# Weight sums of an output projection: from VectorE in the stage to GpSimd in an earlier stage, through DRAM

## The chip, the cores and the metric

One Trainium2 chip, one of its cores; float32 throughout. The metric is the device time of one execution in microseconds (us), the median of the runs shown.

## What is computed

One step of a hybrid trunk layer for 640 tokens (512 of a prompt, 8 x 16 of samples): attention heads and a state-space group side by side, an output projection of both, a SwiGLU feed-forward and a gated embedding. What matters here, cut from the reference:

```python
a = rms_norm(x, g_mix)
proj = a @ w_in
...
merged = jnp.concatenate([rms_norm(attn, g_attn_out), rms_norm(ssm, g_ssm_out)], axis=-1)
h = x + merged @ w_out
f = rms_norm(h, g_ffn)
h = h + (jax.nn.silu(f @ w_gate) * (f @ w_up)) @ w_down
gate = jax.nn.sigmoid(rms_norm(h, g_ple) @ w_ple_gate)
h = h + gate * (p_i @ w_ple_proj)
```

`w_out` has 2048 x 2048 elements. `attn` is 8 heads of 128, `ssm` the gated output of the state-space group (GLU).

## The kernel before, in words

**Products.** Activations stand feature by token, so TensorE holds a 128x128 block of weights and streams 320 tokens. Every float32 operand is split into a high part and a rest (wh, wl of the weights; two planes of each activation), and one product is three matmuls, at L1231, L1232 (both wh) and L1233 (wl). The large projections go by Strassen's scheme in Winograd's form: a 2x2 block product takes seven products instead of eight. Four of the seven left operands are blocks' sums and differences of the weights (`winograd_weights`, L106), the right ones of the activations (`winograd_rows`, L115); `PRODUCTS` (L126) lists for each of the seven which weight operand (0 to 6) meets which activation operand. Operands 0 to 2 are blocks of the weights as they come, 3 to 6 the sums.

**Weights.** `Ring` streams them in units. A unit of the output projection is one [128, 1024] block of float32 (512 KB): four blocks of 256 columns. SyncE loads it to a staging tile wst (two of them, L60). `split` (L67) then has VectorE make the four sums ws (L109 to L112), ScalarE cast wst and ws to wh (L86) and VectorE take the rests wl (L87). wh and wl have two buffers each, ws one. A unit of kind 0 (not Strassen) is only split, at L77 and L78.

**Stages.** The state-space inputs (to about 200 us), v and the scan (to 326), the heads (326 to 658), GLU (663 to 755), the embedding's projection pj (755 to 790), the output projection o (790 to 1024.5), gate and up (to 2125), down, and the last projection p. In the heads TensorE's stream is `feature_major` (L760), the q and k products of one head after another; every four k-blocks it pumps `side` and `side2`, generators that issue the attention of the head before and the norms piece by piece. GLU is `feature_major` as well. The heads' loads stand on SyncE's queue in program order: weights wst, one-hot rows oh, values vp, cached keys kc (L887) and cached values vc (L896), two vc tiles per head that follow each other in one buffer.

**Output projection.** `mk` holds the eight right operands km0 to km7 (each with its seven combinations and its two planes), which `build` (L1082) makes: a load mb or bm, a scaling (L1085), casts (L1076 on ScalarE) and rests (L1077 on VectorE), the sums of rows by L118 to L121. Each of 8 columns j takes 4 units, 42 matmuls each, in `products` (L1219); `strassen` (L1252) then gathers the seven PSUM banks to ro, the residual is added (L1306), and c (L1293), h_dr (L1316) and fc_dr (L1196) follow. The order of instructions on each engine is fixed when the program is built, by a scheduler; an engine's queue is worked in that order, and an instruction that waits holds all behind it.

Of the kernel before, what the change touches and what calls it, by code (L numbers as in the profile page):

```python
# [42 lines left out]
class Ring:  # L43
# [4 lines left out]
    def __init__(self, nc, stage_pool, units):  # L48
        self.nc, self.units, self.sp = nc, units, stage_pool
        self.pool = None  # L50
        self.loaded, self.st, self.cut, self.pos = 0, {}, {}, 0

    def load(self, upto):
        while self.loaded < min(upto, len(self.units)):
            i = self.loaded
            _, src = self.units[i]
            t = self.sp.tile([P, W1], F32, tag="w_st", name=f"wst{i}", bufs=STAGE)
            n = src.shape[1]
            for part in self.parts(i, n):
                self.nc.sync.dma_start(t[:, part], src[:, part])  # L60
            self.st[i] = (t, n)
            self.loaded += 1

    def parts(self, i, n):
        return [slice(0, n // 2), slice(n // 2, n)] if i == 0 else [slice(0, n)]

    def split(self, i):  # L67
# [23 lines left out]

    def ahead(self):
        for j in (self.pos, self.pos + 1):
            if j < len(self.units) and self.units[j][0] == 1:
                self.split(j)

    def next(self):
        i = self.pos
        self.pos += 1
        self.split(i)  # L100
        if i + 1 < len(self.units) and self.units[i + 1][0] == self.units[i][0]:
# [63 lines left out]
def hybrid_step(ctx: ExitStack, tc: tile.TileContext, io):  # L165
# [7 lines left out]
    side, side2 = Side(), Side()  # L173
# [9 lines left out]
    units += [(1, io["w_out"][j, u]) for j in range(8) for u in range(4)]  # L183
# [23 lines left out]

    def act_tile(name):
        return ap_.tile([P, 7, NTOK], F32R, tag="act", name=name)

    def act_rows(name, n):

        ts = [act_tile(f"{name}{i}") for i in range(-(-2 * n // 7))]
        return [tuple(ts[(2 * k + i) // 7][:, (2 * k + i) % 7] for i in range(2)) for k in range(n)]
# [7 lines left out]
    warm = cp.tile([P, 1], F32, name="warm")  # L222
    nc.scalar.activation(warm, ones[:, 0:1], AF.Copy)

    def load_const(name, eng=nc.gpsimd):
        src = io[name]
        t = cp.tile(list(src.shape), F32, name="c_" + name)
# [53 lines left out]
    rtok = cp.tile([P, MT], F32, name="rtok")  # L281
    epsr = mp.tile([P, NTOK], F32, name="epsr")
    negc = mp.tile([40, NTOK], F32R, name="negc")
    negp = mp.tile([P, 512], F32R, name="negp")
# [252 lines left out]
    gffn = load_const("g_ffn")  # L537
    gple = load_const("g_ple")
# [221 lines left out]
    def feature_major(ps, ks, rate=1.0, start=True, stop=True, parts=None):  # L760

        n = len(ks)
        for u in range(0, n, 8):
            wh, wl = ring.next()
            for j in range(min(8, n - u)):
# [7 lines left out]
                if j % 4 == 3:  # L773
                    side2.pump(1.0)
                    side.pump(rate)
# [57 lines left out]
    def forget():  # L833
# [35 lines left out]
        nc.vector.memset(negc.bitcast(F32), 0.0)  # L869
# [6 lines left out]
    def loads(h):  # L876
        oh = tp.tile([P, 2, P], F32, tag="oh", name=f"oh{h}", bufs=1)
        ohr = tp.tile([P, 2, P], F32R, tag="ohr", name=f"ohr{h}", bufs=1)
# [155 lines left out]

    for h in range(H):
# [119 lines left out]
    build_early(4)  # L1155
    at.close()
# [23 lines left out]
    xp = open_top("ffn")  # L1180
    KB = 2
# [37 lines left out]
    def products(name, kps, after=None, order=None):  # L1219
# [4 lines left out]
        def product(i, u, cut):  # L1224
            a, b = PRODUCTS[i]
            wh, wl = cut
# [326 lines left out]
```

## Time and profile before

| | us |
|---|---|
| Runs: median of 3 (lowest, highest) | 2935.68 (2934.81, 2939.37) |
| The profiled execution's own time | 2942.17 |
| Its span | 2940.4 |
| TensorE busy in it (share) | 2828.1 (96%) |
| VectorE busy | 2241.3 (76%) |
| ScalarE busy | 1241.2 (42%) |
| GpSimd busy | 360.3 (12%) |

The profile is one execution; its span is the time between its first and last instruction. Matmuls are pipelined, so that a matmul's own duration (0.31 us) is longer than the distance to the next one. A group of instructions is one line, one engine and one operation; "idle before, releaser" is what ended the engine's wait. PE is TensorE, PEld its weight loads, DVE VectorE, ACT ScalarE, POOL GpSimd, SPq SyncE's queue of DMA issues.

### The profile page before, as it was taken

How to read it: one execution, taken by the hardware profiler on the slowest of the kernel's cores; microseconds unless marked ns; L12 is line 12 of the kernel's file. 1: busy time of each engine (PE TensorE's matmuls, PEld its weight loads, DVE VectorE, ACT ScalarE, POOL GpSimd, SP SyncE). 2: the span in 40 equal slices, each digit the busy share in tenths (PEclk: the TensorE clock that was granted, in tenths of full speed). 3: DMA queues.
4: the chain of work that ended last, by engine and by line, in shares of the span. 5: the costliest groups of instructions: out<-in, count | busy, mean ns of one | idle time of the engine just before them, and what ended most of it. 6: DMA issues, size and time to landing. Idle time of an engine off the chain costs nothing. (4 is left out here: it accounts for less than half of the span.)

```text
span 2940.4 us, 47366 instructions
## 1 busy us (share of the span) xinstructions
PE 2828.1 (96%) x19051; PEld 2716.3 (92%) x19051; DVE 2241.3 (76%) x3629; ACT 1241.2 (42%) x1628; POOL 360.3 (12%) x405
## 2 busy tenths in 40 slices
PE   8999999999889889999999999999999999999998
PEld 6889988887789889999999999999999999998898
DVE  7758254445688888888888888888887777899888
ACT  5343355556644453333333333333433344345433
POOL 1213300001000001101111111111110110100011
PEclk9999999999999999999999999999999999999999
DMA  5666734546545623232323333333555455647444
GB/s 174 168 187 179 244 118 169 182 156 239 205 141 180 240 98 125 95 124 96 119 101 118 102 118 102 118 102 118 205 145 148 135 158 170 164 158 273 136 158 140
DMA packets 137484, 449.16 MB, mean 153 GB/s; under 512 B 14096, under 2 KB 34672, under 8 KB 124464
## 3 DMA queue, kind: packets, MB, share of 16 engines
q1 hardware_dynamic: 120032, 396.47, 39.9%
q0 software_dynamic: 15936, 45.47, 6.1%
q10 hardware_dynamic: 1296, 4.20, 0.4%
q8 instruction: 149, 2.44, 0.3%
q14 instruction: 71, 0.58, 0.1%
HBM read 342.25 MB, written 101.18 MB: 151 GB/s over the span
## 5 line engine op out<-in xcount | busy, mean ns | idle before, releaser
L86 ACT ACTIVATE wh<-wst 128x768 fp32r<-128x768 f32 x328 | 276.9, 845 | 660.0 <-issue 320.0
L87 DVE TENSOR_TENSOR wl<-ws,wh 128x1024 fp32r<-128x1024 f32 x328 | 423.6, 1291 | 102.1 <-ACT wh L86 101.7
L86 ACT ACTIVATE wh<-ws 128x1024 fp32r<-128x1024 f32 x328 | 344.6, 1051 | 358.0 <-DVE ws L112 357.9
L87 DVE TENSOR_TENSOR wl<-wst,wh 128x768 fp32r<-128x768 f32 x328 | 334.3, 1019 | 169.8 <-ACT wh L86 169.7
L1231 PE MATMUL d<-kt,wh 128*128 128x320 f32 x1232 | 383.5, 315 | 11.7 <-ACT wh L86 5.4
L1231 PE MATMUL g<-kf,wh 128*128 128x320 f32 x1232 | 382.4, 311 | 5.5 <-ACT wh L86 5.3
L1232 PE MATMUL g<-kf,wh 128*128 128x320 f32 x1232 | 381.8, 310 | 0.0
L1232 PE MATMUL d<-kt,wh 128*128 128x320 f32 x1232 | 380.6, 312 | 0.0
L1231 PE MATMUL u<-kf,wh 128*128 128x320 f32 x1232 | 380.1, 309 | 0.0
L1233 PE MATMUL g<-kf,wl 128*128 128x320 f32 x1232 | 375.7, 310 | 4.5 <-DVE wl L87 4.5
L1232 PE MATMUL u<-kf,wh 128*128 128x320 f32 x1232 | 380.0, 309 | 0.0
L1233 PE MATMUL u<-kf,wl 128*128 128x320 f32 x1232 | 376.2, 309 | 0.1
L1233 PE MATMUL d<-kt,wl 128*128 128x320 f32 x1232 | 344.5, 315 | 7.3 <-DVE wl L87 7.3
L1231 PEld LDWEIGHTS d<-kt,wh 128*128 128x128 f32 x1232 | 234.9, 191 | 17.9 <-ACT wh L86 10.2
L1231 PEld LDWEIGHTS g<-kf,wh 128*128 128x128 f32 x1232 | 232.7, 189 | 6.8 <-ACT wh L86 6.8
L1233 PEld LDWEIGHTS g<-kf,wl 128*128 128x128 f32 x1232 | 230.3, 188 | 5.6 <-DVE wl L87 5.3
L1232 PEld LDWEIGHTS d<-kt,wh 128*128 128x128 f32 x1232 | 235.0, 191 | 0.0
L1233 PEld LDWEIGHTS d<-kt,wl 128*128 128x128 f32 x1232 | 224.7, 191 | 11.1 <-DVE wl L87 10.6
L1232 PEld LDWEIGHTS g<-kf,wh 128*128 128x128 f32 x1232 | 232.9, 189 | 0.0
L1231 PEld LDWEIGHTS u<-kf,wh 128*128 128x128 f32 x1232 | 231.3, 188 | 0.0
L1232 PEld LDWEIGHTS u<-kf,wh 128*128 128x128 f32 x1232 | 231.3, 188 | 0.0
L1233 PEld LDWEIGHTS u<-kf,wl 128*128 128x128 f32 x1232 | 230.2, 188 | 0.4 <-DVE wl L87 0.4
(488 smaller groups left out, 5878.4 us busy)
## 6 DMA issues: line engine op xcount, KB each, us to landing
wst<-in_w_gate SPq DMA_DIRECT2D x88, 512.0 KB
wst<-in_w_up SPq DMA_DIRECT2D x88, 512.0 KB
wst<-in_w_down SPq DMA_DIRECT2D x88, 512.0 KB
tc_dr<-t SPq DMA_DIRECT2D x22, 1120.0 KB
kt<-tc_dr SPq DMA_DIRECT2D x22, 1120.0 KB
wst<-in_w_qk SPq DMA_DIRECT2D x32, 512.0 KB
kc<-in_cache_k SPq DMA_DIRECT2D x16, 1024.0 KB
vc<-in_cache_v SPq DMA_DIRECT2D x16, 1024.0 KB
```

The source lines that it names most:

```text
L86: a = nc.scalar.activation(wh[:, part], x, AF.Copy)
L87: b = nc.vector.tensor_tensor(wl[:, part], x, wh[:, part].bitcast(F32), op=OP.subtract)
L1231: nc.tensor.matmul(ps[i], wh[:, a, w], k[:, 0, b], start=f, stop=False)
L1232: nc.tensor.matmul(ps[i], wh[:, a, w], k[:, 1, b], start=False, stop=False)
L1233: nc.tensor.matmul(ps[i], wl[:, a, w], k[:, 0, b], start=False, stop=l)
```

## The change

The 32 units of `w_out` become units of kind 2. Their four sums are made by GpSimd in 64 steps of a new generator, `sum_weights`, which is pumped beside `side2`: 56 pumps in heads 1 to 7, 16 in GLU. A step loads half the columns of a unit's four blocks ([128, 4, 128], 256 KB, rows of 512 bytes) into a tile `pre` (two buffers) on SyncE's queue, and the step after it makes the four sums in place on GpSimd and stores them to a DRAM tensor `s_dr` on GpSimd's queue. In the output projection a unit's blocks 1 to 3 are loaded (128x768), and the sums as two more tiles wt of 128x512, of which there are three buffers. wh and wl are then made in three parts (768, 512, 512 columns). The sums stand in another order, which `SUMS` maps. To find room, some constants move to a pool that ends before the output projection, and negc, negp and ohr into unused rows of an activation tile.

```diff
     def load(self, upto):
         while self.loaded < min(upto, len(self.units)):
             i = self.loaded
-            _, src = self.units[i]
+            kind, src = self.units[i]
+            src = src[0] if kind == 2 else src
             t = self.sp.tile([P, W1], F32, tag="w_st", name=f"wst{i}", bufs=STAGE)
             n = src.shape[1]
-            for part in self.parts(i, n):
+            for part in self.parts(i, n) if kind < 2 else [slice(256, n)]:
                 self.nc.sync.dma_start(t[:, part], src[:, part])
...
+    def load_sums(self, i):
+        if i < len(self.units) and self.units[i][0] == 2 and i not in self.sums:
+            self.sums[i] = []
+            for h in range(2):
+                s = self.pool_of_sums(2).tile([P, 2, 256], F32, tag="w_s2", name=f"wt{i}_{h}", bufs=3)
+                self.nc.sync.dma_start(s, self.units[i][1][1][:, 2 * h : 2 * h + 2])
+                self.sums[i].append(s)
...
-            s = self.pool.tile([P, 4, 256], F32, tag="w_s", name=f"ws{i}", bufs=1)
             q = t.rearrange("p (q n) -> p q n", q=4)
-            winograd_weights(nc, q, s)
-            for part, x in ((slice(0, 3), q[:, 1:]), (slice(3, 7), s)):
+            if self.units[i][0] == 1:
+                s = self.pool_of_sums(1).tile([P, 4, 256], F32, tag="w_s", name=f"ws{i}", bufs=1)
+                winograd_weights(nc, q, s)
+                parts = [(slice(3, 7), s)]
+            else:
+                self.load_sums(i)
+                parts = list(zip((slice(3, 5), slice(5, 7)), self.sums.pop(i)))
+            for part, x in [(slice(0, 3), q[:, 1:])] + parts:
                 a = nc.scalar.activation(wh[:, part], x, AF.Copy)
                 b = nc.vector.tensor_tensor(wl[:, part], x, wh[:, part].bitcast(F32), op=OP.subtract)
             self.done = (a.ins, b.ins)
-        self.cut[i] = (wh, wl)
+        self.cut[i] = (wh, wl) if self.units[i][0] == 0 else (wh, wl, SUMS[self.units[i][0]])
+        if self.units[i][0]:
+            self.load_sums(i + 1)
         self.load(i + 1 + STAGE)
...
+def winograd_weights_in_place(eng, q):
+
+    tt = eng.tensor_tensor
+    tt(q[:, 3], q[:, 0], q[:, 3], op=OP.add)
+    tt(q[:, 0], q[:, 1], q[:, 0], op=OP.subtract)
+    tt(q[:, 1], q[:, 3], q[:, 1], op=OP.subtract)
+    tt(q[:, 2], q[:, 2], q[:, 1], op=OP.subtract)
+
+
+
+SUMS = {1: (0, 1, 2, 3, 4, 5, 6), 2: (0, 1, 2, 6, 4, 3, 5)}
...
-    units += [(1, io["w_out"][j, u]) for j in range(8) for u in range(4)]
+    s_dr = dp.tile([32, P, 4, 256], F32, name="s_dr")
+    units += [(2, (io["w_out"][j, u], s_dr[4 * j + u])) for j in range(8) for u in range(4)]
...
                 if j % 4 == 3:
                     side2.pump(1.0)
+                    side3.pump(1.0)
                     side.pump(rate)
...
+    def sum_weights():
+
+        last = None
+        for i in range(65):
+            if i < 64:
+                n = slice(P * (i % 2), P * (i % 2) + P)
+                t = tp.tile([P, 4, P], F32, tag="pre", name=f"pre{i}", bufs=2)
+                nc.sync.dma_start(t, io["w_out"][i // 8, i // 2 % 4].rearrange("p (q n) -> p q n", q=4)[:, :, n])
+            if last is not None:
+                t_, i_, n_ = last
+                winograd_weights_in_place(nc.gpsimd, t_)
+                nc.gpsimd.dma_start(s_dr[i_][:, :, n_], t_)
+            last = t, i // 2, n
+            yield
+
+    side3.add(sum_weights())
     for h in range(H):
...
+    side3.drain()
     at.close()
     mid.close()
     psB.close()
...
         def product(i, u, cut):
             a, b = PRODUCTS[i]
-            wh, wl = cut
+            wh, wl, places = cut
+            a = places[a]
```

How the built order changes, at two places. In the rows of the changed kernel the line numbers are its own: L62 is L60 of before, L920 is L879, L923 is L882, L928 is L887, L937 is L896, and L1083 is the load of a pre tile.

SyncE's queue in the heads, where one head's cached values and the next weights are issued. Before:

```order
L60 DMA wst_4510<-in_w_qk 128x1024 [waits DMAHW7_49,DVE_49]
L60 DMA wst_4637<-in_w_qk 128x1024 [waits DMAHW0_49,DVE_49]
L882 DMA vp_4691<-v_dr 128x5x128 [waits DMAHW4_49,PE_49]
L896 DMA vc_1_4565<-in_cache_v 128x2048 [waits DMAHW5_49,PE_49]
L896 DMA vc_0_4693<-in_cache_v 128x2048 [waits DMAHW6_49,DMAHW5_49,PE_49]
L60 DMA wst_4729<-in_w_qk 128x1024 [waits DMAHW2_49,DVE_49]
L887 DMA kc_0_4772<-in_cache_k 128x2048 [waits PE_49]
```

And in the changed kernel (DMASW is a store on GpSimd's queue):

```order
L62 DMA wst_5256<-in_w_qk 128x1024 [waits DMAHW5_49,DMAHW2_49,DVE_49]
L923 DMA vp_5331<-v_dr 128x5x128 [waits PE_49]
L1083 DMA pre_5227<-in_w_out 128x4x128 [waits DMAHW0_49,DMASW7_49,Pool_49]
L937 DMA vc_1_5185<-in_cache_v 128x2048 [waits PE_49]
L1083 DMA pre_5282<-in_w_out 128x4x128 [waits DMAHW1_49,DMAHW6_49,DMASW0_49,Pool_49]
L62 DMA wst_5369<-in_w_qk 128x1024 [waits DMAHW7_49,DVE_49]
L1083 DMA pre_5321<-in_w_out 128x4x128 [waits DMAHW4_49,DMASW1_49,Pool_49]
L937 DMA vc_0_5333<-in_cache_v 128x2048 [waits DMAHW5_49,PE_49]
```

Loads of pre tiles now stand ahead of the cached values and between the weights, and each of them waits for a store on GpSimd's queue.

VectorE's queue ahead of the output projection, where the first unit's wl is made (wl_7751 before; wl_8190 after). Before:

```order
L1077 TENSOR_TENSOR km_7186<-mb_7184,km_7186 128x320
L111 TENSOR_TENSOR ws_7752<-ws_7752,wst_7419 128x256
L87 TENSOR_TENSOR wl_7751<-wst_7419,wh_7750 128x768
L112 TENSOR_TENSOR ws_7752<-wst_7419,ws_7752 128x256
L1077 TENSOR_TENSOR km_7186<-ms_7185,km_7186 128x960
L78 TENSOR_TENSOR wl_7518<-wst_7332,wh_7517 128x1024
L118 TENSOR_TENSOR ms_7367<-mb_7366 128x320
L87 TENSOR_TENSOR wl_7751<-ws_7752,wh_7750 128x1024
L1085 TENSOR_TENSOR mb_7437<-mb_7437,ssqa 128x1280
```

In the changed kernel (L107 is L87, L1134 is L1077, L1142 is L1085, L153 to L156 are L118 to L121; km_8108, km_8138 and km_8153 are km4, km5 and km6):

```order
L156 TENSOR_TENSOR ms_8107<-ms_8107,mb_8106 128x320
L1134 TENSOR_TENSOR km_8108<-mb_8106,km_8108 128x320
L1134 TENSOR_TENSOR km_8108<-ms_8107,km_8108 128x960
L153 TENSOR_TENSOR sm_8137<-bm_8139 128x320
L154 TENSOR_TENSOR bm_8139<-bm_8139 128x320
L155 TENSOR_TENSOR sm_8137<-bm_8139,sm_8137 128x320
L1134 TENSOR_TENSOR km_8153<-bm_8154,km_8153 128x960
L156 TENSOR_TENSOR sm_8137<-sm_8137,bm_8139 128x320
L1134 TENSOR_TENSOR km_8138<-bm_8139,km_8138 128x320
L107 TENSOR_TENSOR wl_8190<-wt_0_8194,wh_8189 128x512
L107 TENSOR_TENSOR wl_8190<-wt_1_8196,wh_8189 128x512
```

The wl of the first unit's sums has moved from among the builds of km0 to km2 to behind those of km0 to km4 and parts of km5 and km6. On TensorE, 24 matmuls (products 1 and 2 of the first two units) stand ahead of the first product that takes a sum.

## Rows read from the trace of the kernel before

**Rows 1.** Windows: busy us (instructions) of each engine, granted clock, DMA share, GB/s.
```profile
400.00:450.00 50.00, 50.00 (x377) 42.27 (x376) 26.73 (x46) 30.25 (x46) 2.64 (x5) 1.00 0.56 201
...
790.00:800.00 10.00, 1.57 (x10) 1.30 (x9) 8.56 (x15) 7.71 (x11) 0.00 (x0) 0.72 0.78 271
800.00:804.70 4.70, 4.70 (x19) 4.70 (x20) 4.70 (x5) 1.01 (x1) 0.00 (x0) 0.50 0.61 238
804.70:816.00 11.30, 11.30 (x79) 11.30 (x79) 11.30 (x20) 4.80 (x7) 0.00 (x0) 1.00 0.13 46
816.00:840.00 24.00, 17.31 (x87) 13.82 (x87) 21.58 (x36) 11.21 (x15) 0.00 (x0) 0.93 0.26 77
...
870.00:1005.00 135.00, 127.03 (x855) 125.06 (x854) 113.50 (x191) 57.14 (x69) 4.37 (x5) 1.00 0.50 178
...
1024.50:1060.00 35.50, 25.50 (x145) 23.17 (x145) 33.67 (x48) 19.75 (x21) 0.87 (x1) 0.90 0.40 153
...
1100.00:1150.00 50.00, 50.00 (x343) 50.00 (x342) 42.11 (x69) 18.68 (x22) 10.59 (x8) 1.00 0.33 110
```

**Rows 2.** Waits from 755 to 1030: total us, times, longest.
```profile
ACT wh L86 <- DVE ws L112: 37.6, 13, 3.7
```

**Rows 3.** Groups by line and shape, 845 to 1010: busy us, mean ns.
```profile
L87 DVE TENSOR_TENSOR wl<-ws,wh 128x1024 fp32r<-128x1024 f32 x24 | 32.1, 1337 | 12.4 <-ACT wh L86 12.4
...
L109 DVE TENSOR_TENSOR ws<-wst 128x256 f32<-128x256 f32 x25 | 10.5, 419 | 0.2
```

**Rows 4.** Waits from 860 to 1010.
```profile
PE o L1231 <- ACT wh L86: 8.0, 6, 1.3
```

**Rows 5.** Timeline, 938 to 953, ScalarE and TensorE: start, duration, idle before.
```profile
947.91 1.55 ACT L1293 ACTIVATE c<-ro,c_g_ffn 128x640 f32<-128x640 f32 x2 [5.27 <-DVE ro L1306]
...
951.40 0.42 PE L1231 MATMUL o<-km,wh 128*128 128x320 f32 x1 [1.34 <-ACT wh L86]
```

**Rows 6.** Timeline, 786 to 842, VectorE and TensorE.
```profile
797.70 0.82 DVE L244 SCALAR_TENSOR_TENSOR ssq<-rzs,rys 128x640 f32<-128x640 f32 x1
...
800.90 2.89 DVE L1085 TENSOR_TENSOR bm<-bm,ssq 128x1280 f32<-128x1280 f32 x2
...
805.85 1.15 DVE L1077 TENSOR_TENSOR km<-bm,km 128x960 fp32r<-128x960 f32 x1
806.92 0.49 DVE L119 TENSOR_TENSOR mb<-mb 128x320 f32<-128x320 f32 x1
...
799.72 0.64 PE L1231 MATMUL o<-km,wh 128*128 128x320 f32 x1 [8.43 <-ACT pje L1147]
```

**Rows 7.** The instructions on qk: ns min/median/max, first and last start.
```profile
L771 PE MATMUL qk<-a,wh x1024: 305/309/603, 326.3 to 656.8; 128*128 128x320 f32 x171
```

**Rows 8.** GpSimd's groups by shape, whole trace.
```profile
L121 POOL TENSOR_TENSOR t<-t 128x320 f32<-128x320 f32 x22 | 32.5, 1477 | 1.7
...
L1031 POOL TENSOR_TENSOR ssqa<-ssqa,aT 128x640 f32<-128x640 f32 x7 | 10.9, 1557 | 0.5
...
L1266 POOL TENSOR_TENSOR ro<-ro,qo 128x320 f32<-128x320 f32 x8 | 7.0, 875 | 257.0 <-DVE ro L1263 257.0
```

**Rows 9.** Timeline, 780 to 806: a weight's load and its first reader.
```profile
779.93 0.33 SPq L60 DMA_DIRECT2D wst<-in_w_out  x1
...
783.87 0.85 ACT L86 ACTIVATE wh<-wst 128x768 fp32r<-128x768 f32 x1 [2.05 <-DMA wst<-in_w_out]
```

**Rows 10.** DMA issues: KB each, median us from issue to landing.
```profile
d_dr<-D POOLq DMA_DIRECT2D x16, 256.0 KB, 5.7
...
o_kT<-qkT POOLq DMA_DIRECT2D x8, 320.0 KB, 3.2
```

**Rows 11.** Waits from 326 to 755, for cached values.
```profile
PE pv L1016 <- DMA vc<-in_cache_v: 2.6, 2, 1.6
```

**Rows 12.** Timeline, 1294 to 1299: VectorE beside GpSimd.
```profile
1294.29 1.11 DVE L110 TENSOR_TENSOR ws<-wst 128x256 f32<-128x256 f32 x1
...
1294.18 0.94 POOL L118 TENSOR_TENSOR t<-t 128x320 f32<-128x320 f32 x1 [5.22 <-DVE t L1343]
```

More of the change, by code (lines that the diff above doesn't have):

```diff
@@ L51, in __init__ @@
         self.loaded, self.st, self.cut, self.pos = 0, {}, {}, 0
+        self.sums, self.sum_pool, self.sum_kind = {}, None, 0
     def load(self, upto):
@@ L65, in parts, with pool_of_sums @@
         return [slice(0, n // 2), slice(n // 2, n)] if i == 0 else [slice(0, n)]
+    def pool_of_sums(self, kind):
+        if self.sum_kind != kind:
+            self.sum_kind, self.sum_pool = kind, self.open_sums()
+        return self.sum_pool
+    def load_sums(self, i):
[5 more added lines that the diff above has]
+                self.sums[i].append(s)
     def split(self, i):
@@ L93, in ahead @@
         for j in (self.pos, self.pos + 1):
-            if j < len(self.units) and self.units[j][0] == 1:
+            if j < len(self.units) and self.units[j][0]:
                 self.split(j)
@@ L100, in next @@
         self.split(i)
-        if i + 1 < len(self.units) and self.units[i + 1][0] == self.units[i][0]:
+        if i + 1 < len(self.units) and bool(self.units[i + 1][0]) == bool(self.units[i][0]):
             self.split(i + 1)
@@ L172, in hybrid_step @@
     dp = ctx.enter_context(tc.tile_pool(reuse_waits="tile", name="dram", bufs=1, space=DRAM))
-    side, side2 = Side(), Side()
+    side, side2, side3 = Side(), Side(), Side()
     units = []
@@ L206, in hybrid_step @@
     t_dr = dp.tile([64, 1], F32, name="t_dr")
+    spare = []
     def act_tile(name):
@@ L213, in act_rows @@
         ts = [act_tile(f"{name}{i}") for i in range(-(-2 * n // 7))]
+        if name == "a":
+            spare.append(ts[-1])
         return [tuple(ts[(2 * k + i) // 7][:, (2 * k + i) % 7] for i in range(2)) for k in range(n)]
@@ L220, in hybrid_step, with load_const @@
     ones = onesr.bitcast(F32)
-    warm = cp.tile([P, 1], F32, name="warm")
+    warm = mp.tile([P, 1], F32, name="warm")
     nc.scalar.activation(warm, ones[:, 0:1], AF.Copy)
-    def load_const(name, eng=nc.gpsimd):
+    def load_const(name, eng=nc.gpsimd, pool=mp):
         src = io[name]
-        t = cp.tile(list(src.shape), F32, name="c_" + name)
+        t = pool.tile(list(src.shape), F32, name="c_" + name)
         eng.dma_start(t, src)
@@ L278, in hybrid_step @@
     load_x(3)
-    rtok = cp.tile([P, MT], F32, name="rtok")
+    rtok = mp.tile([P, MT], F32, name="rtok")
     epsr = mp.tile([P, NTOK], F32, name="epsr")
-    negc = mp.tile([40, NTOK], F32R, name="negc")
-    negp = mp.tile([P, 512], F32R, name="negp")
+    negc, negp = spare[0][:40, 4], spare[0][:, 5, :512]
     fz = mp.tile([P, MT, 8], F32, name="fz")
@@ L536, in hybrid_step @@
     gso = load_const("g_ssm_out")
-    gffn = load_const("g_ffn")
-    gple = load_const("g_ple")
+    gffn = load_const("g_ffn", pool=cp)
+    gple = load_const("g_ple", pool=cp)
     bglu = load_const("b_glu")
@@ L868, in forget @@
         nc.vector.tensor_tensor_scan(c[:, 512:], keep, row[:, 512:], 0.0, op0=OP.mult, op1=OP.add)
-        nc.vector.memset(negc.bitcast(F32), 0.0)
+        nc.vector.tensor_scalar(negc, ones[:40, 0:1].to_broadcast([40, NTOK]), 0.0, None, op0=OP.mult)
         nc.scalar.activation(negc[0:8], c, AF.Copy, scale=-1.0)
@@ L877, in loads @@
         oh = tp.tile([P, 2, P], F32, tag="oh", name=f"oh{h}", bufs=1)
-        ohr = tp.tile([P, 2, P], F32R, tag="ohr", name=f"ohr{h}", bufs=1)
+        ohr = spare[0][:, 6, : 2 * P].rearrange("p (a n) -> p a n", a=2)
         nc.sync.dma_start(oh, io["onehot"][h])
@@ L1180, in hybrid_step, with open_sums @@
     xp = open_top("ffn")
+    sums = ExitStack()
+    def open_sums():
+        nonlocal sums
+        sums.close()
+        sums = ctx.enter_context(ExitStack())
+        return sums.enter_context(tc.tile_pool(reuse_waits="tile", name="sums", bufs=1))
+    ring.open_sums = open_sums
     KB = 2
```

## The prediction

> **What bounds the kernel now.** I read the page first, which shows TensorE busy almost throughout: a change that only moves work of other engines can gain no more than TensorE's stalls in its stage, and loses what it makes TensorE wait elsewhere. Then windows by stage, which show where the stalls are [rows 1], the waits of the output projection, and the groups of its lines. In the heads (400 to 450) TensorE is busy 50.00 of 50 us with VectorE at 26.7 and GpSimd at 2.6, so VectorE and GpSimd are free there, but there is nothing to gain, only to lose. In the output projection (790 to 1024.5) there are three kinds of stall. At its start TensorE is busy 1.57 of 10 us, then 17.31 of the 24 us from 816, with VectorE at 21.58. From 870 to 1005 it is busy 127.03 of 135. Behind its end, at the start of gate, it is busy 25.50 of 35.5. A steady matmul comes every 50 / 343 = 0.1458 us (window 1100 to 1150). The longest wait of ScalarE's casts says whose fault it is: wh waits 37.6 us for the last sum, L112 [rows 2].
>
> **What goes from VectorE.** One unit's four sums and its wl of 1024 columns [rows 3] go: 4 x 0.42 + 1.34 = 3.0 us, where two wl of 512 take their place, about 1.34 in all with one more start. So VectorE gains some 1.6 us per unit, 50 us over 32 units. TensorE gets of that only what it waits for: it stalls only where VectorE is late. I take the three places in turn.
>
> *Six stalls inside the stage.* In the window 860 to 1010 TensorE waits 8.0 us, six times, for ScalarE's wh [rows 4]. The timeline shows one [rows 5]: ScalarE's c starts at 947.91, after 5.27 us of waiting for ro, the wh is queued behind c, and TensorE goes on at 951.40 after 1.34. Between the end of the column's products and ro VectorE now has two sums and half a wl of 1024 columns less in front: ro comes 0.84 + 0.67 = 1.5 us sooner, which is all that the wait needs. Against it: on the SyncE queue the load of a third unit's second half of sums stands behind the store of h, which waits for the same ro. I take 6 of the 8 us, bounds 0 and 8: **-6**.
>
> *The end of the stage.* Two fewer sets of sums stand before gate's first units, but kf loads (1120 KB each) and their casts are what ScalarE waits for there too. Of the 10.0 us of idle TensorE in that window [rows 1] I take 4, a little more than the 2 x 1.6 that two units are worth since each also frees ScalarE's wait, bounds 0 and 8: **-4**.
>
> *The start.* Here the order matters more than the amount. Before, the first unit's wl of its sums stands among the builds of km0 and km1, and TensorE does whole units as the km come. After, it stands behind the builds of km0 to km4 and parts of km5 and km6, and TensorE has only products 1 and 2 of two units (24 matmuls) ahead of the first product that needs a sum. The distance in VectorE's row, from the end of the second rsqrt (L244) on: four L1085 at 1.45, seven km of 960 at 1.07, and fifteen instructions of 320 columns at 0.41 (0.49 less the 0.08 by which the next one starts early), by such rows [rows 6]: 5.8 + 7.5 + 6.2 = 19.5 us. L244 ended at 798.5; ten sums and two wl less come ahead of it, 5.7 us at most, if ScalarE's rsqrt steps don't hold it: 793 to 798.5, I take 795. So the first sum is ready at about 815 (wl itself overlaps the first products), bounds 812 and 818. Then 144 matmuls of the first column remain, 21.0 us; after such a wait TensorE runs at half clock (19 matmuls in 4.70 us at 0.50 behind the 8.43 us wait, [rows 1, 6]), 1.9 us more, and I add 2 for the next units' wl: 840. Before, 195 matmuls were done by 840 (10 + 19 + 79 + 87 in the four windows), so the 168 of the first column by about 836. That is **+4**, bounds -1 and +9. VectorE's smaller load doesn't help as long as TensorE is the late one.
>
> **What comes into the heads.** 64 steps, each a load of 256 KB, four sums of 128x128 on GpSimd, a store of 256 KB in pieces of 512 bytes; two buffers, so load i waits for the landing of store i-2. One step per pump. Pace: head 0 makes no pump, its 192 matmuls end by 326.3 + 28 = 354.3, and heads 1 to 7 make 56 pumps by 656.8 [rows 7]: 5.4 us each. A buffer may therefore take 10.8 us from load to landed store. Its parts:
> - the sums: GpSimd's instruction costs 875 ns for 320 columns and 1557 for 640 [rows 8], so 2.13 ns per column over 193: 466 for 128, four in a row with their semaphores 2.1 us.
> - the load: a weight of 512 KB issued at 779.93 had its reader start at 783.87 [rows 9]: 3.9 us. With half the bytes in pieces of 512 bytes I keep 3.9.
> - the store: the same size and pieces took 5.7 at the median (d_dr), and in the heads o_kT took 3.2 [rows 10]. I take 5.0, nearer the row of the same shape; the ends are 3.2 and 5.7.
>
> With 0.2 of waiting: 3.9 + 2.1 + 5.0 + 0.2 = 11.2 us, 5.6 per step, 0.2 over the pace. Over 56 steps the chain falls 11 us behind. This is no matter for the sums, which have until 795, but the loads stand in SyncE's queue among the heads' own: a load of sums that waits for a store holds the second cache_v load and the next weight, as the order shows. Weights stand two ahead; cache_v doesn't: TensorE already waits for it, up to 1.6 us [rows 11]. So what the chain lags, TensorE waits: **+11**. The low end is 9.4 us per buffer, no lag, 0; the high end, with the 5.7 and sums stretched by 1477 / 875 (L121, which runs beside VectorE, against the same shape alone, [rows 8]), is 13.2 us, 6.6 per step, 67 us. The added bytes, 64 x 512 KB, on DMA engines that are busy for 0.56 [rows 1], speak for the upper half.
>
> *VectorE beside GpSimd.* A sum of 128x256 that takes 0.42 us [rows 3] takes 1.11 while GpSimd runs an instruction of its own [rows 12]. GpSimd's 256 sums are 120 us; half of that meets a VectorE that is idle, and what is stretched grows its 26.7 of 50 us [rows 1] to some 32, still covered. I cost it at **+2** for softmax steps that come late, bounds 0 and 5; rival 4 is what it costs if that cover doesn't hold.
>
> GpSimd's own queue gets 64 issues of stores and the sums in front of its other stores. It is busy 2.6 of 50 us there [rows 1] and some 20 with the sums: nothing. The moved constants are loaded and read as before: nothing.
>
> **Sum**, against the profiled execution of 2942.17 us: -6 - 4 + 4 + 11 + 2 = +7, 2949.2. The median of the runs, 2935.68, lies 6.5 lower; in it the same +7 gives **2942.7 us**, slower. About 0.2%, 5.9 us, is what a measurement tells from no change.
>
> **Rivals.**
> 1. *The chain keeps the pace* (the other side). If stores land in under 4.6 us, a buffer takes under 10.8 and nothing in the heads waits. Then the terms are 0 to +2 for the heads, the better ends inside the stage and at its end (-8, -6), and about 0 for the start, since the chain was done long before and VectorE comes early to the sums: -12, 2923.7. For it: o_kT's 3.2 in the heads. Against: its rows are 2560 bytes. Chance 0.22.
> 2. *Given back.* At 10.95 us per buffer the lag is 4 us and the sum is 0: 2935.7. Within 5 us of it there is no change to be seen. Chance 0.16.
> 3. *The lag takes over.* At 12 us per buffer (stores at 5.5, sums stretched by VectorE to 0.53) each step is 0.6 late: 34 us, and the sum +30: 2966. For it: the d_dr row, the added DMA, the stretched sums of [rows 12]. Against: a late head also slows the pumps' demand, and weights have room. Chance 0.15.
> 4. *VectorE late in the heads.* About 56 x 2.1 = 118 us of sums fall there; VectorE meets them for 26.7 / 50 of it, 63 us, and at 0.42 for 1.11 [rows 3, 12] loses 39 us, 5 per head. If a third of that reaches TensorE through the softmax steps it is 13 instead of 2, the sum +18: 2953.7. Chance 0.05. The Trainium skill gives the rule behind it (GPSIMD Engine Reference, Specifications): GpSimd's interface to SBUF is shared with VectorE, and contends with instructions that have two SBUF inputs. By that rule the reads of PSUM and the reductions among the softmax steps go free, which speaks for the third or less; the trace agrees for a sum of two SBUF inputs, 0.42 against 1.11 us.
> 5. My forecast, +1 to +14 with the chain slightly late. Chance 0.42.
>
> **How the numbers follow.** Faster by over 0.2% is rival 1: 0.22. No change: rival 2 and the forecast below +5.9, 0.16 + 0.12 = 0.28. Slower: the forecast above that, 0.30, and rivals 3 and 4: 0.50. The range has to reach into both: from 2922, which leaves out the best third of rival 1, to 2968, which leaves out half of rival 3: some 0.15 in all. The forecast's own range is 2937 to 2950.
>
> **What would show it.** Right: in the heads TensorE below 50.00 of 50 us with waits for vc, and SyncE's loads of sums waiting for s_dr stores; stores landing near 5 us; a wait of about 13 us on the first o_3 after 24 matmuls; no six stalls for wh. Wrong: heads at 50.00 with loads of sums issued at the pumps' pace (rival 1); stores over 6 us (rival 3); or sums of the first units ready before 808, which would turn the start's term into a gain of several microseconds.

## The result, and the profile after

The change makes the kernel slower: 2975.28 us (median of 4 runs, 2969.45 to 2981.61) against 2936.3 (4 runs, 2934.81 to 2939.37), a ratio of 1.0132 [1.0106, 1.0157]. The forecast, 2942.7 with 2922 to 2968, has the sign right and the size wrong: +39 us where it said +7, and outside its range. The profiled execution is one of 2981.61 us, span 2979.8; the one of before has span 2940.4, so the traces differ by 39.4 us, about as the medians do.

I cut both traces at TensorE's first and last matmuls of each stage, in us:

| stretch | before | after | difference |
|---|---|---|---|
| up to the first qk | 326.3 | 329.1 | +2.8 |
| qk (heads 0 to 7) | 331.1 | 361.4 | **+30.3** |
| from there to GLU's first matmul | 5.9 | 13.8 | **+7.9** |
| GLU (the last head beside it) | 92.1 | 98.8 | **+6.7** |
| up to the output projection's first matmul | 34.8 | 38.0 | +3.2 |
| output projection | 234.5 | 224.4 | **-10.1** |
| start of gate (to 1/22 of its matmuls) | 66.1 | 62.2 | **-3.9** |
| the rest, to the last matmul | 1841.0 | 1843.7 | +2.7 |

So the stage that the change is about gives back more than the 6 us that were forecast (10.1 and 3.9, less the 3.2 ahead of it), and the heads and GLU lose 45 us where 13 were forecast.

The engines' busy time on the page after:

```profile
PE 2833.6 (95%) x19051; PEld 2727.4 (92%) x19051; DVE 2207.1 (74%) x3533; ACT 1247.1 (42%) x1661; POOL 553.8 (19%) x725
```

GpSimd has 194 us more and VectorE 34 less. Neither is TensorE's bound; the loss is not in these sums. The windows after (columns as in [rows 1]), the heads and the middle of the output projection:

```profile
400.00:450.00 50.00, 43.96 (x304) 37.49 (x302) 29.15 (x45) 29.75 (x42) 32.41 (x50) 1.00 0.58 189
600.00:650.00 50.00, 46.46 (x329) 41.73 (x329) 20.48 (x34) 22.96 (x36) 26.46 (x45) 0.93 0.69 234
...
870.00:1005.00 135.00, 135.00 (x913) 135.00 (x912) 92.63 (x144) 64.96 (x97) 4.37 (x5) 0.99 0.71 242
```

In the heads TensorE falls from 50.00 of 50 to 43.96, with VectorE and GpSimd both far from full: they wait too. From 870 to 1005 the picture of [rows 1] is turned round: 135.00 of 135 where it was 127.03, with VectorE at 92.6 instead of 113.5. The six stalls are gone.

What the engines wait for in the heads and GLU (waits from 326 to 800; us in total, times, longest):

```profile
POOL pre L140 <- DMA pre<-in_w_out: 154.2, 45, 8.2
...
PE pv L1057 <- DMA vc<-in_cache_v: 31.6, 7, 9.3
...
ACT Ps L946 <- DMA m_dr<-ag: 26.9, 5, 7.4
...
ACT g L1107 <- DMA gld<-g_dr: 25.3, 5, 10.1
```

The cached values of [rows 11] were waited for for 2.6 us, twice; now for 31.6, seven times. ScalarE's Ps now waits for the store m_dr of the head before, which shares its buffer: the store goes out 1.2 to 4.9 us after its data (ag) are ready, where it took 0.3 before. Why they are late stands in SyncE's own queue (340 to 780):

```profile
SPq L1083 <- DMA s_dr<-pre: 203.6, 51, 9.7
SPq L62 <- DVE wl L93: 70.3, 14, 10.1
```

51 of the 64 loads of w_out (L1083) wait at the head of SyncE's queue until a store has landed, 4 us each, and everything behind them waits too. Some eight of these waits fall behind 690, when the heads' products end: there TensorE waits 10.9 us for cached values and 7.9 for GLU's inputs (690 to 805), where it waited 2.6 and 2.5 before. The timeline shows two such waits (a start and a duration that includes the wait); the cached values stand behind the second:

```profile
423.94 0.55 SPq L1083 DMA_DIRECT2D pre<-in_w_out  x1
424.58 1.20 SPq L62 DMA_DIRECT2D wst<-in_w_qk  x1
425.83 0.42 SPq L920 DMA_DIRECT2D oh<-in_onehot  x1
426.35 8.61 SPq L1083 DMA_DIRECT2D pre<-in_w_out  x2
...
435.01 0.61 SPq L62 DMA_DIRECT2D wst<-in_w_qk  x1
438.89 6.17 SPq L1083 DMA_DIRECT2D pre<-in_w_out  x2
...
445.83 0.46 SPq L937 DMA_DIRECT2D vc<-in_cache_v  x1
```

The Trainium skill states what lies behind this (DMA: Bandwidth & Descriptors, Anatomy of one DMA — SWDGE (gpsimd) path): DMA engines do not wait on semaphores, the wait is the issuing sequencer's, before dispatch. The trace agrees, on SyncE's queue too: 203.6 us of waits for s_dr.

The stores landed in 3.9 us at the median (5.0 was taken):

```profile
s_dr<-pre POOLq DMA_DIRECT2D x64, 256.0 KB, 3.9
m_dr<-ag POOLq DMA_DIRECT2D x8, 320.0 KB, 7.9
```

VectorE is slowed in the heads as well. Groups by line and shape from 380 to 640, before and then after:

```profile
L78 DVE TENSOR_TENSOR wl<-wst,wh 128x1024 fp32r<-128x1024 f32 x25 | 30.5, 1221 | 22.8 <-ACT wh L77 18.2 <-issue 4.5
...
L924 DVE SCALAR_TENSOR_TENSOR z<-pm,epsr 128x640 f32<-128x640 f32 x13 | 10.7, 819 | 11.4 <-PE pm L922 11.4
```

```profile
L93 DVE TENSOR_TENSOR wl<-wst,wh 128x1024 fp32r<-128x1024 f32 x22 | 31.8, 1445 | 8.6 <-ACT wh L92 4.9 <-issue 3.6
L969 DVE TENSOR_TENSOR qkT<-xg,z 128x640 f32<-128x640 f32 x12 | 10.8, 904 | 0.4
...
L965 DVE SCALAR_TENSOR_TENSOR z<-pm,epsr 128x640 f32<-128x640 f32 x12 | 9.8, 816 | 6.9 <-PE pm L963 6.7
```

A wl with two inputs in SBUF takes 1445 ns on average instead of 1221; the z that reads PSUM takes 816 as before (819).

Theory at this point: the heads pay for loads that hold their queue, plus VectorE slowed by GpSimd's reads. Rivals: the lag of the chain's mean pace (the prediction's own reason), and the added DMA bytes by themselves.

### The profile page after: what moved, and what is told of

It is laid out like the page before. It is cut to its first block, busy times and chain, and to the rows that moved or that the text cites. A ratio compares the mean times of both kernels' runs of the same rounds, so it can differ in the third digit from the quotient of the medians.

```text
span 2979.8 us, 47955 instructions
## 1 busy us (share of the span) xinstructions
PE 2833.6 (95%) x19051; PEld 2727.4 (92%) x19051; DVE 2207.1 (74%) x3533; ACT 1247.1 (42%) x1661; POOL 553.8 (19%) x725
## 5 line engine op out<-in xcount | busy, mean ns | idle before, releaser
L107 DVE TENSOR_TENSOR wl<-wst,wh 128x768 fp32r<-128x768 f32 x328 | 335.0, 1021 | 198.6 <-ACT wh L106 198.3
L107 DVE TENSOR_TENSOR wl<-ws,wh 128x1024 fp32r<-128x1024 f32 x296 | 381.1, 1288 | 98.4 <-ACT wh L106 97.5
L106 ACT ACTIVATE wh<-ws 128x1024 fp32r<-128x1024 f32 x296 | 311.2, 1051 | 329.4 <-DVE ws L134 329.0
L1301 PE MATMUL g<-kf,wl 128*128 128x320 f32 x1232 | 369.1, 311 | 3.6 <-DVE wl L107 3.6
L1301 PE MATMUL u<-kf,wl 128*128 128x320 f32 x1232 | 368.7, 309 | 0.0
```

The lines of the kernel that those rows point to most:

```text
L1301: nc.tensor.matmul(ps[i], wl[:, a, w], k[:, 0, b], start=False, stop=l)
```

## The experiments

Thirteen kernels ran. Ratios are against the kernel before, run on the same chip. "qk" is the stretch of the table above in the profiled execution (331.1 before, 361.4 after), "vc" TensorE's wait for cached values in the heads and GLU (2.6 before, 31.6 after). Half-widths behind a "±" below are worked out from the intervals of the two ratios that are compared.

| run | us | ratio [interval] | qk | vc |
|---|---|---|---|---|
| e1 loads on GpSimd's queue | 2972.44 | 1.0115 [1.009, 1.0139] | 353.2 | 5.1 |
| e3 stage only | 2932.87 | 0.9972 [0.9963, 0.9982] | 331.1 | 2.5 |
| e4 transfers, no sums | 2962.81 | 1.0078 [1.0057, 1.0098] | 366.8 | 33.0 |
| e5 sums, no transfers | 2944.78 | 1.0017 [1.0002, 1.0032] | 343.4 | 6.2 |
| f1 no sums, all on GpSimd's queue | 2956.14 | 1.0065 [1.0047, 1.0083] | 353.7 | 5.2 |
| f2 half the sums | 2952.44 | 1.0047 [1.0033, 1.0061] | 345.7 | 13.1 |
| f3 sums on VectorE | 2972.97 | 1.0114 [1.0094, 1.0134] | 364.6 | 5.8 |
| f4 memsets for sums | 2934.16 | 0.9983 [0.9973, 0.9992] | 332.6 | 3.8 |
| g1 copies alone | 3013.92 | 1.0257 [1.0239, 1.0274] | 332.6 | 2.6 |
| g2 copies and sums | 3022.05 | 1.0285 [1.027, 1.03] | 342.8 | 3.4 |
| g3 column's work later | 2932.32 | 0.9976 [0.9966, 0.9987] | 332.7 | 3.6 |
| g4 copies tied to the heads | 2943.59 | 1.0005 [0.9991, 1.0019] | 334.8 | 8.2 |
| g5 the tie alone | 2933.28 | 0.9976 [0.9964, 0.9987] | 332.7 | 2.8 |

**e3: the output projection alone.** No side job; the projection loads plain blocks in the sums' place.

```
-    units += [(2, (io["w_out"][j, u], s_dr[4 * j + u])) ...
+    units += [(2, (io["w_out"][j, u], io["w_out"][j, u].rearrange(...))) ...
-    side3.add(sum_weights())
```

> No sums are made and nothing is added to the heads; the output projection takes plain weight blocks in place of the sums (loaded as the changed kernel loads the sums), so the projection computes something else. What is left is the change in the output projection alone. All three theories put the whole loss in the heads and GLU, so this is faster than before by what the traces show of the projection and of gate's start, 10 + 2 us: 2922 to 2927. My recorded terms for this part (-6 inside, -4 at the end, +4 at the start) would be 2930. If a part of the loss were in the projection it would be at or above 2936.

Measured -0.28%, 8.2 us, and qk at 331.1 exactly as before: this is what the stage is worth when its sums cost nothing, nearer to the 6 of the recorded terms than to the 12 expected from the two traces. From the end of GLU to the start of gate it takes 38.5 + 224.6 + 62.7 = 325.8 us against 34.8 + 234.5 + 66.1 = 335.4. So the whole change costs 1.32 + 0.28 = 1.60%, 47 us (± 8), in what comes before.

**e4: loads and stores without the sums.**

```
-                winograd_weights_in_place(nc.gpsimd, t_)
```

> The loads and the stores stay on their queues, but GpSimd's four instructions between them are left out, so the blocks are stored unsummed. A buffer's cycle of 12.8 us loses the 3.3 us of the sums, 9.5, under the 10.8 that the pumps leave. Theory A: the loads no longer lag, vc waits under 5 us, 2925 to 2934. Theory B: the same bytes, 2965 to 2976. Theory C: VectorE is undisturbed, 2925 to 2930 as well; the next run separates it from A.

Against e3 the transfers alone cost 1.06%, 31 us (± 7), near what theory B expected; what the bytes by themselves cost is left to g4. The 64 loads go out between 353.3 and 656.1 us, one every 4.8:

```profile
L1083 SPq DMA_DIRECT2D pre<-in_w_out x64: 539/545/622, 353.3 to 656.1; - x64
```

That is faster than a pump every 5.4, so by the prediction's rule of the mean pace the heads lose nothing. They lose 31 us, with the same waits (326 to 690):

```profile
SPq L1083 <- DMA s_dr<-pre: 170.1, 54, 8.5
...
PEld pv L1057 <- DMA vc<-in_cache_v: 30.6, 5, 13.0
...
PE pv L1057 <- DMA vc<-in_cache_v: 28.6, 4, 12.7
```

The mean pace falls as the reason: 54 of the 64 loads wait for a store although they go out faster than the pumps. The pumps don't pace SyncE: it comes to a load of w_out early and stands there until the store has landed. What goes, as I read it, is the lead with which it issued the heads' own loads. With the loads all out by 656, GLU and the gap ahead of it lose 2 us here, not the 15 of the changed kernel.

**e5: the sums without transfers.** GpSimd makes the same 256 sums on a zero tile that stays in SBUF; the projection loads plain blocks as in e3, here and in f4, g1, g2, g4 and g5.

```
+        still = tp.tile([P, 4, P], F32, tag="pre", name="pre", bufs=1)
+        nc.gpsimd.memset(still, 0.0)
...
-                nc.sync.dma_start(t, io["w_out"]...)
+                t = still
...
-                nc.gpsimd.dma_start(s_dr[i_][:, :, n_], t_)
```

> GpSimd's 256 instructions stay at their pumps, on one resident tile of zeros; the added loads and stores of the heads are left out, and the projection takes plain weight blocks in place of the sums. Theory A and B: nothing holds the loads, so as with the projection alone, 2922 to 2930. Theory C: VectorE is stretched as in the changed kernel, 2960 and more.

Against e3 the sums cost 0.45%, 13 us (± 5), between the two expectations, and qk grows by 12.3. VectorE's groups, 380 to 640:

```profile
L93 DVE TENSOR_TENSOR wl<-wst,wh 128x1024 fp32r<-128x1024 f32 x24 | 31.4, 1307 | 21.4 <-ACT wh L92 18.1 <-issue 3.3
L957 DVE TENSOR_TENSOR sl<-sq,sh 128x640 fp32r<-128x640 f32 x13 | 12.5, 960 | 2.9 <-ACT sh L956 2.8
...
L965 DVE SCALAR_TENSOR_TENSOR z<-pm,epsr 128x640 f32<-128x640 f32 x13 | 10.6, 818 | 9.1 <-PE pm L963 9.1
```

sl (822 ns in e3) is 17% longer, wl 7%, z not at all. These means mix two stretches, since the sums end at 524.6: from 380 to 450 wl takes 1439 ns and sl 1063, from 525 to 640 they take 1222 and 821. In the changed kernel the sums last through the window and beyond, to 771.5. Rival 4's mechanism is there. But its price, a third of 39 us, is met by luck: over qk VectorE is busy only 9.2 us longer than in e3. The windows of qk, of e3 and then of e5:

```profile
326.10:657.20 331.10, 328.75 (x2413) 290.96 (x2411) 150.15 (x246) 176.63 (x266) 28.97 (x49) 1.00 0.47 165
...
324.00:667.40 343.40, 333.71 (x2413) 294.64 (x2411) 159.31 (x246) 176.86 (x266) 175.79 (x306) 0.99 0.46 159
```

And there is a second route. From 420 to 520 GpSimd is busy 18.2 to 18.5 of every 20 us, its sums stand in front of its own stores, and the second m_dr goes out 13.4 us after its ag is ready (timeline, 485 to 512):

```profile
491.70 0.83 ACT L1067 ACTIVATE ag<-aT,c_g_attn_out 128x640 f32<-128x640 f32 x1
...
505.90 0.56 POOL L1073 DMA_DIRECT2D m_dr<-ag  x1
...
508.47 0.79 ACT L946 ACTIVATE Ps<-ss,nm 128x640 f32<-128x640 f32 x1 [8.24 <-DMA m_dr<-ag]
...
509.41 0.63 PE L962 MATMUL pm<-sh,onesr 128*128 128x320 f32 x1 [4.29 <-ACT Ps L946]
```

Counted from the first qk, this ag comes 5.5 us later than in e3 and the next one 12.3 later; behind it nothing more is lost in qk. So over half of the 12.3 falls in the one head with this wait. How much of the rest is VectorE's stretch no run separates.

**f4: memsets in place of the sums.** As e5, with four memsets of 512 columns per step, so that GpSimd is nearly as busy (164.7 us in qk, 175.8 in e5) but reads nothing.

```
-                winograd_weights_in_place(nc.gpsimd, t_)
+                for _ in range(4):
+                    nc.gpsimd.memset(t_, 0.0)
```

> As the run with sums alone, but GpSimd writes the resident tile four times per step (memset of 512 columns, about 0.5 us each by 0.97 for 1024) instead of adding: as busy, reading nothing. Sums alone cost 12 us against the projection alone. If GpSimd's reads of SBUF hold VectorE's two-input instructions: wl back to 1.22 us from 1.31 and the q and k stage to 331 to 335 from 343.4, before -7 to -2. If any access does, or the order in which the instructions stand: 340 and more, before +3 to +7.

GpSimd's memsets take 118.9 us between 380 and 640, and qk is 332.6, 1.5 above e3, as expected for reads that hold VectorE:

```profile
L1088 POOL MEMSET pre<- 128x512 f32 x223 | 118.9, 533 | 11.8
```

```profile
L93 DVE TENSOR_TENSOR wl<-wst,wh 128x1024 fp32r<-128x1024 f32 x24 | 29.3, 1222 | 22.3 <-ACT wh L92 18.0 <-issue 4.1
...
L948 DVE TENSOR_SCALAR P<-P,sm 128x512 f32<-128x512 f32 x6 | 6.5, 1076 | 0.2
```

wl is at 1222 again. So it is GpSimd's reading that stretches VectorE's two-input instructions, not its being busy. The Trainium skill has this rule (SBUF — State Buffer, SBUF: two separate sides): a VectorE instruction with two SBUF inputs contends for a shared port pair only with a GpSimd operation that reads SBUF. The trace agrees, 1307 against 1222. For the time f4 decides less. Its memsets are shorter (533 ns, where e5's sums take 549 to 607), GpSimd keeps up, and the same m_dr goes out 0.3 us after its ag, so both of e5's routes are gone at once.

**e1 and f1: the loads moved to GpSimd's queue,** with the sums (e1) and without (f1).

```
-                nc.sync.dma_start(t, io["w_out"]...)
+                nc.gpsimd.dma_start(t, io["w_out"]...)
```

> The only edit: the loads of weight blocks to be summed are issued on GpSimd's queue instead of SyncE's, so that their wait for a stored buffer holds GpSimd, not the heads' own loads. Same bytes, same sums. Theory A (order of the queue: loads that wait for a store hold cached values and GLU's inputs behind them): TensorE's waits for vc fall from 31.6 us to under 5, the heads and GLU come to within 10 us of before, and the time to 2925 to 2934. Theory B (traffic: the added bytes make the DMA engines late): bytes are the same, so vc stays late and the time at 2965 to 2976. Theory C (GpSimd's sums slow VectorE in the heads): the sums are the same, so 2965 to 2976.

> Loads and stores of all 64 steps, both on GpSimd's queue, and no sums between them. Theory A' (a load that waits for a store's landing stands in SyncE's queue in front of the second cached values, so TensorE waits whenever the two meet, whatever the mean pace): SyncE's queue is free, the q and k stage back to 331 to 338 us from 366.8, vc waits under 5 us, the time before -6 to +2. Theory B (traffic of the DMA engines): same bytes as the run without sums, so 360 us and more in that stage, before +18 to +28.

SyncE is free, and cached values are waited for for 5 us only; but qk stays at 353, far above what the theory of SyncE's held queue alone gives: the times of both runs came out as theory B expected, though vc did not stay late. In e1 there is also a loss behind the heads: 57.7 us between GLU and the output projection (38.6 in e3), whose last sums are made at 827.8. In f1 the hold has moved along (waits from 326 to 690):

```profile
POOL s_dr L1086 <- DMA pre<-in_w_out: 102.7, 47, 6.2
POOL pre L1083 <- DMA s_dr<-pre: 91.6, 43, 6.8
...
ACT Ps L946 <- DMA m_dr<-ag: 40.9, 5, 12.0
...
PE pm L962 <- ACT Ps L946: 10.1, 2, 6.9
```

GpSimd's queue now stands still for 194 us, the heads' own stores (m_dr) land late behind it, ScalarE waits for them for 40.9 us (26.9 in the changed kernel, no such wait in e3), and TensorE for ScalarE. Against e3, f1 costs 0.93%, 27 us (± 6), not told apart from e4's 31. What these two runs leave open is how much of it the bytes would cost with no wait at all.

**f3: the sums on VectorE,** transfers as in f1.

```
-                winograd_weights_in_place(nc.gpsimd, t_)
+                winograd_weights_in_place(nc.vector, t_)
```

> The sums of the 64 steps on VectorE instead of GpSimd, loads and stores on GpSimd's queue. VectorE gets 256 instructions of 128 columns, about 75 us in 430 in which it is idle for half. If GpSimd's arithmetic is what slows the heads (theory C, 12 of the 30 us), and its queue the rest (A'), both are gone: the q and k stage at 331 to 340, the time before -6 to +4. If a busier VectorE is as bad for the attention steps as a stretched one: stage at 343 and more, before +6 to +15.

No better than after, and outside both expectations: qk 364.6. The sums are cheaper there (289 ns instead of 576), but VectorE itself now stands in its own queue for loads, before the softmax steps:

```profile
L140 DVE TENSOR_TENSOR pre<-pre 128x128 f32<-128x128 f32 x40 | 11.6, 289 | 55.8 <-DMA pre<-in_w_out 55.8
```

**f2: half the dose.** Only the last four columns take their sums from the side job, 32 steps at every other pump.

```
+    units += [(1, io["w_out"][j, u]) for j in range(4) for u in range(4)]
...
-        for i in range(65):
+        for i in range(32, 65):
...
+            yield
```

> Only the units of the last four columns get their sums ahead: 32 steps instead of 64, one in two pumps; the first four columns are as before. A buffer then has 21 us for a cycle of 13. A': a load hardly ever waits, vc waits under 5 us; VectorE's stretch is halved: +6 in the heads; the projection gains what three of its six inner stalls and its end give, -6, and its start is as before: before -3 to +4. B: half the traffic's cost, before +8 to +15. If GpSimd's sums cost by themselves what the run with sums alone showed, 12 us, half of that is the +6.

Half the steps cost 14.6 us in qk, half of 30.3, with 13.1 us for cached values. The time, 0.47% or 14 us above the kernel before, is in the range expected of the traffic (8 to 15), not of the held queue (-3 to 4); but that expectation took it that a load hardly ever waits. The pace wasn't halved: the 32 loads go out between 349.9 and 546.4, one every 6.3 us, as fast as buffers come free, and 29 of them wait 4.0 us each for a store:

```profile
SPq L1084 <- DMA s_dr<-pre: 116.2, 29, 9.8
```

So in these two doses the cost goes with the number of steps. The output projection gains 2.0 us of its 10 for it.

**g1 and g2: the bytes without the waits, and with the sums.** Per step two copies from DRAM to DRAM, one on each queue; g2 adds the sums on a resident tile.

```
+                nc.sync.dma_start(s_dr[i // 2][:, :, n], src)
...
+                nc.gpsimd.dma_start(s2_dr[i_][:, :, n_], src_)
...
+                winograd_weights_in_place(nc.gpsimd, still)
```

The last line is g2's alone.

> Per step of the side job there are two copies of 256 KB from w_out to DRAM (512-byte pieces, one on SyncE's queue at the place of the load, one on GpSimd's at the place of the store) and nothing else: the bytes and pieces of the loads and stores, but no buffer, so no transfer waits for another. The sums are left out, and the output projection reads plain blocks of w_out in their place, so the output is not the reference's. Theory of the held queue (a load that waits for a store's landing holds what stands behind it): the qk stage takes what it takes without any side job, about 331 to 336 us, cache_v waits stay under 4 us, total 2930 to 2938. Rival (the added bytes and pieces by themselves slow the heads' own loads): the qk stage stays near the 354 us of the run with both transfers on GpSimd's queue, total 2950 to 2958.

> As the kernel of copies alone, and GpSimd makes its four sums per step as well, on a zero tile that stays in SBUF (their results are used by nobody; the output projection reads plain blocks, so the output is not the reference's). If the price of GpSimd's reads stands by itself, this is the copies' kernel plus the 12 us that the sums cost without any transfer: 2942 to 2950 by the held queue, qk near 344; if bytes and sums make each other worse, the step from copies to copies with sums is over 16 us, and wl of 1024 columns takes over 1340 ns on average in the qk stage, where the sums alone gave 1300. By the rival of bytes: 2960 to 2970.

As a test of the bytes in the heads g1 failed: a copy that waits for nothing isn't held to its place either, and the scheduler put the copies at the program's start (4 to 141 us). The first qk starts at 408.3 instead of 326.3, and qk is at 332.6 since no copy was left for it. g2's copies ran there too, so it doesn't show what bytes and sums do to each other. It repeats e5: the sums cost 0.28%, 8 us (± 7), and 10.2 in qk, with the same wait (12.2 us of ScalarE for m_dr, 5.1 of TensorE for ScalarE).

**g4 and g5: copies tied to the heads, and the tie alone.** The same two copies per step, both on GpSimd's queue behind a tiny GpSimd copy of the current weight; g5 has only the tie.

```
+            a = nc.gpsimd.tensor_copy(gate, paced[0][:, :4].bitcast(F32))
+            with tc.issue_after(a.ins):
+                nc.gpsimd.dma_start(s_dr[i // 2][:, :, n], src)
+                nc.gpsimd.dma_start(s2_dr[i // 2][:, :, n], src)
```

> Per step one tiny GpSimd copy of four columns of the heads' current weight, which comes when that weight is cut, and behind it on GpSimd's queue two copies of 256 KB from w_out to DRAM in 512-byte pieces: the bytes, pieces and queue of the run with loads and stores on GpSimd's queue, at the heads' own pace, but no copy waits for another to land. The sums are left out and the output projection reads plain blocks of w_out, so the output is not the reference's. Held queue: the qk stage returns to 331 to 337 us, total 2930 to 2939. Bytes: the qk stage stays at 348 to 356 us, total 2947 to 2958. In between, both have their part, by the share of the 22 us that stays.

> As the kernel of paced copies, without the copies: only the tiny GpSimd copy per step is left, which ties GpSimd to the heads' weights. The sums are left out and the output projection reads plain blocks of w_out, so the output is not the reference's. Both theories: as the run of the stage alone, qk stage 331 to 334 us, total 2931 to 2936. If it is more than 3 us above that, the tie itself holds GpSimd's queue, and that much has to come off the run with the copies.

The tie costs nothing: g5 is at 0.9976, as e3. The copies cost 0.29% over it, 8.5 us (± 5), between the two expectations, with 5 us more of waits for cached values (8.2 against 2.8); f1, with the same bytes, pieces and queue but with waits, costs 27 over e3. The windows 380 to 640, of f1 and then of g4, show DMA equally loaded, 256 and 257 GB/s, and TensorE at 247.7 and 254.5 of 260:

```profile
380.00:640.00 260.00, 247.68 (x1810) 215.65 (x1809) 121.06 (x190) 136.16 (x204) 92.50 (x130) 0.97 0.76 256
```

```profile
380.00:640.00 260.00, 254.45 (x1878) 220.84 (x1877) 126.03 (x205) 144.09 (x217) 106.74 (x170) 0.99 0.73 257
```

So both theories have their part, and the held queue has the larger: about 18 of f1's 27 us are the waits, about 9 the bytes. The split isn't sharp: the 18 has 8 us to either side; the copies go from DRAM to DRAM, where f1's transfers go through SBUF, and no run separates that; and g4's profiled execution was one of its fastest, 2935.29, with qk only 2.1 us above g5, while its runs reach from 2934.92 to 2951.03; where the longer ones spend it no trace here shows.

**g3: the stalls without any sums.** The kernel before, where the work on a finished column is issued behind the weights of the next column's third unit.

```
+            if u == 1 and rest:
+                with tc.issue_after(ring.done[0]), tc.issue_after(ring.done[1]):
+                    rest.pop()()
```

> The kernel before without any side job; only the work on a finished column of the output projection (ScalarE's c and squares, VectorE's rows of c, the stores) is issued after the weights of the next column's third unit. Nothing is left out. If the six stalls inside the stage are ScalarE's casts of weights queued behind a c that waits for ro, they go without a single sum moved from VectorE: 5 to 8 us less, ratio 0.9973 to 0.998, PE o <- wh waits from 860 to 1010 under 2 us. Rival: VectorE has too much work per unit, whatever stands in front; then the waits come back one unit later and the time stays within 2 us of the kernel before.

Measured 0.9976, about 7 us less, and as fast as e3, though no sum was moved. The windows 870 to 1005, of g3:

```profile
870.00:1005.00 135.00, 135.00 (x923) 135.00 (x922) 116.96 (x203) 59.68 (x72) 4.71 (x5) 1.00 0.53 189
```

TensorE is at 135.00 of 135 with VectorE at 117.0, more than the 113.5 of [rows 1]. VectorE had the time all along; the six stalls were the order, a cast of weights queued behind a c that waits. g3 is the version that beats both kernels.

## Why the prediction was wrong

*The output projection: six stalls -6, start +4, end -4.* Right in kind, and near in size. The stage in two windows, cut where its first stalls end, before:

```profile
790.20:860.00 69.80, 54.68 (x323) 50.66 (x322) 63.55 (x102) 33.69 (x44) 0.88 (x1) 0.90 0.44 154
860.00:1024.70 164.70, 153.03 (x1026) 150.18 (x1025) 138.21 (x227) 71.76 (x86) 5.25 (x6) 1.00 0.54 197
```

and after:

```profile
841.10:900.00 58.90, 38.94 (x230) 38.18 (x230) 51.27 (x75) 32.20 (x48) 0.86 (x1) 0.80 0.57 187
900.00:1065.50 165.50, 165.50 (x1129) 165.26 (x1127) 108.80 (x168) 77.35 (x113) 5.27 (x6) 1.00 0.75 265
```

At the start TensorE is idle for 69.80 - 54.68 = 15.1 us before and 20.0 after: +4.9 for the +4. It is the wait that was described, once, for the first sum (waits from 800 to 1110):

```profile
PE o L1299 <- ACT wh L106: 15.4, 1, 15.4
```

VectorE's row from the end of the second rsqrt (845.50) to the first wl of sums (866.62) is 21.1 us, where 19.5 was worked out. Behind the start the idle time goes from 11.7 us to none: the 8.0 of the six stalls whole, where 6 was taken, and 3.7 at the end. With 3.9 at gate the end gives 7.6 for the 4, and 3.2 ahead of the stage and 2.7 in the rest, which no term had, take that back. The stage's 10.1 us are these 6.8 us less of idle time and 3.3 us less of busy time (204.4 for 207.7), which no term had either. The sum of the stage, -6, is e3's -8.

*VectorE beside GpSimd, +2, and GpSimd's own queue, nothing.* Together 13 (e5 against e3). Both were covered by average room: VectorE at 26.7 of 50 us, GpSimd at "some 20". VectorE's instructions were stretched, by 9.2 us in all where rival 4 took 39. GpSimd's queue wasn't nothing: its sums came in a row, and over half of the 12.3 us of qk falls in the head where one store stood behind them. Rival 4 named 13 us, at a chance of 0.05, but by a third of a stretch four times too large; that the number came out is luck.

*The chain's lag, +11.* This is the step that failed: "A buffer may therefore take 10.8 us from load to landed store." The parts were near (loads 4.0 us at the median for 3.9, as e1 shows them, stores 3.9 for 5.0; GpSimd's sums 551 to 605 ns in the heads for 466), but the rule from them to TensorE was wrong. e4 keeps the pace and loses 31 us; f2 has half the steps and loses half. What costs is the loads that wait at the head of a queue and what stands behind them: 31 us over 64 steps, half a microsecond each, of which by g4 some 9 us are the bytes. Rival 1, whose chain keeps the pace, had this wrong in the same way: "nothing in the heads waits" is not what e4 shows.

The parts add up: stage -8 (e3), transfers +31 (e4 over e3), sums +13 (e5 over e3), together +36 of the measured 39.

*Signs named ahead:* TensorE below 50.00 of 50 with waits for vc, loads that wait for stores of s_dr, a wait of some 13 us on the first o_3 (15.4) and no six stalls: all there. Stores near 5 us were not, and the loads' pace, which was to tell rival 1, tells nothing of TensorE (e4).

## What to carry to other kernels

A load that may have to wait for a buffer must not stand in an in-order queue ahead of loads that are needed just in time: here it cost the queue's lead although the mean pace was kept (e4), and another queue only moved the wait to that queue's customers (f1). Work put on an idle GpSimd isn't free: what it reads from SBUF stretches VectorE's two-input instructions, and what it does stands in front of its own stores, though it has room on average. Before work is moved off an engine that is "late", look at what stands in front of it in the queue: here the same stalls went by issuing one column's work a unit later.

## What the runs showed of the hardware that was not expected

- GpSimd's memsets leave VectorE's two-input instructions alone (wl 1222 ns) but stretch a one-input scaling: P of 512 columns takes 1076 ns on average of six beside them, 629 before. Why is not shown. It is the instruction that goes faster than the others per column (550 ns for 640 columns, against 819 to 826 for the two-input steps).
- The same 128x128 sum took about 460 ns on GpSimd at the median, 289 on VectorE, and GpSimd's mean rose to 551 to 605 in the heads: both engines lose where they meet.
- A copy without a buffer has no place of its own, which is the scheduler's doing and not the chip's: 128 copies of 256 KB went ahead of the program's own loads, and the first qk came 82 us later (g1).
